# Two kinds of elementwise work of an encoder layer made on GpSimd instead of VectorE: a weight sum and the low parts of turned activations

## The chip, the cores and the metric

One core of a Trainium2 chip runs the whole program: TensorE (PE, with its weight loads as PEld), VectorE (DVE), ScalarE (ACT), GpSimd (POOL), and SyncE (SP), which issues the DMAs. The metric is the device time of one execution in microseconds, with inputs and outputs in HBM. Times of a run differ a little from execution to execution, so a change of the whole is judged by the median of several, and its stages by one profiled execution.

## The reference

Two layers of an encoder over 256 tokens of width 1024, all in float32. What matters here is how each layer's matmuls are made; the change touches the projection of attention and the FFN.

```python
q, k, v = ...                                   # normed, rotated
branch_b = gqa_attention(q, k, v) @ w_o_attn    # 1024 x 1024
mixed = jax.nn.sigmoid(gate_a) * branch_a + jax.nn.sigmoid(gate_b) * branch_b
h = h + rms_norm(mixed @ w_out, g_mix_post)

gate, up = jnp.split(rms_norm(h, g_ffn_pre) @ w_ffn_in, 2, axis=-1)   # FFN_HIDDEN = 2816
h = h + rms_norm((jax.nn.silu(gate) * up) @ w_ffn_out, g_ffn_post)
```

## The kernel before

**Three matmuls for one.** TensorE takes fp32r operands, so that each float32 operand is split into a high part (a cast on ACT) and a low part (source minus high part, a subtraction on DVE). `split` (L111) makes both, `mm3` (L99) adds three products: high by high, high by low, low by high. 12 matmuls of 512 columns make a half step of this, 24 a whole one.

**The weight stream.** Weights come in units of 128 x 2048 values. `plan` (L175) lists them in the order of use, and `Stream` (L214) loads them: raw buffers (two) by DMA on SP's queue, then for every unit two pieces of 1024 columns, each an ACT cast into `wh` (L113) and a DVE subtraction into `wl` (L109). There are four pairs of `wh` and `wl`, and `fill` (L309) prepares a unit as soon as fewer than `depth` pairs are held; `done` (L321) gives one back when its last matmul is recorded. A raw buffer can be loaded again when the DVE subtraction has read it.

**Groups of seven.** Where two halves of the tokens meet a 2 x 2 arrangement of weight units, seven products stand for eight (`seven`, L611, for the matmuls; `Stream.step`, L289, for the weights). `step` is called for n = 1 to 7 and each time makes one unit ready (`made`, L285). The four units of the group are x, z, y and q. x and z are loaded into a pair of `wh`/`wl` buffers lent for the purpose (tiles named `lent`), y into a large buffer (`big`), q into a raw buffer in step 5. Between the steps units are added to one another over 2048 columns by the helper `add` (L292):

| step | unit made ready | sum made after it, on DVE |
|---|---|---|
| 1 | x | x + z into x |
| 2 | x | x + y into x |
| 3 | x | |
| 4 | y | z + y into z |
| 5 | z | x + q into x |
| 6 | q | |
| 7 | x | |

There is one such group in each layer's merge (the attention projection; `MERGE`, L39) and three in each layer's FFN (`PAIRS`, L40), eight in all. The string `FFN` (L38) is the order of the FFN's steps: u a plain unit, a digit a step of the group of seven, o an output step, which needs the activations of one block of 256 hidden columns and one unit of `w_ffn_out`.

**Turned activations.** The FFN's hidden activations have to be transposed before the output steps. Most are turned by a DMA: `turn_words` (L394) takes each float32 word apart into two 16-bit halves (ACT copy, L404), sends it through a DMA transpose on SP's queue (L410), puts the halves together again (ACT copies, L417 and L423), and calls `Split.put` (L390), which splits the result into high and low part for `mm3`. `far=True` marks the calls from the FFN: in each layer four pieces of 256 columns (the first two blocks, by half of the tokens) and seven of 512 (three plain blocks, and two groups by half of the tokens). The last group's are turned on TensorE instead. `hid.need` makes the output step's matmuls wait until these parts have been recorded.

**Order.** The program's text is not the order of the engines' queues. The compiler orders each engine's instructions by priorities and by its own estimate of when their inputs are ready, so an instruction can stand in its queue well before the place where the text has it; `tc.issue_after` and `tc.high_priority` bend that order in places. On the chip each engine then runs its queue strictly in order and waits for semaphores. GpSimd's own work in the kernel is small: the powers and sums of the norms, the masks of the attention scores, the rope tables (L690, L694) and a few memsets.

Of the kernel before, what the change touches and what calls it, by code (L numbers as in the profile page):

```python
# [10 lines left out]
F32 = mybir.dt.float32  # L11
# [4 lines left out]
ALU = mybir.AluOpType  # L16
AX = mybir.AxisListType

P = 128
T = 256  # L20
# [31 lines left out]
def trunk_kernel(ctx: ExitStack, tc: tile.TileContext, a: dict, out: bass.AP):  # L52
# [7 lines left out]
    nc = tc.nc  # L60
# [13 lines left out]
    def nm(s):  # L74
        uid[0] += 1
        return f"{s}_{part[0]}_{uid[0]}"
# [4 lines left out]
    def mid(dt=F32):  # L81
        return b4p.tile([P, 1024], dt, tag="mid", name=nm("mid"))
# [7 lines left out]
    def t512():  # L90
        return smp.tile([P, 512], F32, tag="t512", name=nm("t512"), bufs=7)
# [16 lines left out]
    def vsub(out, in0, in1):  # L108
        nc.vector.tensor_tensor(out=out, in0=in0, in1=in1, op=ALU.subtract)  # L109

    def split(hi, lo, src):  # L111

        cast = nc.scalar.copy(hi, src)  # L113
        vsub(lo, src, hi.bitcast(F32))
        return cast
# [98 lines left out]
    class Stream:  # L214
# [54 lines left out]
        def put(self, x, parts=2):  # L269

            wh = wp.tile([P, UNIT], F32R, tag="wh", name=nm("wh"))
            wl = wp.tile([P, UNIT], F32R, tag="wl", name=nm("wl"))
            self.ready.append((wh, wl))
            self.held += 1
            cuts = [slice(j * x.n // parts, (j + 1) * x.n // parts) for j in range(parts)]
            return [(wh[:, c], wl[:, c], x.raw[:, c]) for c in cuts]
# [12 lines left out]
        def step(self, n, x, y, z, q):  # L289
            def add(to, other):  # L290
                c = slice(0, 2048)
                nc.vector.tensor_tensor(out=to.raw[:, c], in0=to.raw[:, c], in1=other.raw[:, c], op=ALU.add)  # L292

            if n == 7:
                self.load()
            self.made((x, x, x, y, z, q, x)[n - 1])
            if n == 1:
                add(x, z)
            elif n == 2:
                add(x, y)  # L300
            elif n == 4:
                add(z, y)
            elif n == 5:
                add(x, q)
            elif n == 7:
                self.held -= 1
                self.lend = True
# [55 lines left out]
    class Split:  # L363
# [23 lines left out]
                    kept.append(t)  # L387
            self.makers[hf] = kept

        def put(self, src, k, n, t0, tn):  # L390

            split(*self.at(k, n, t0, tn), src.rearrange("p (k t) -> p k t", t=tn))

        def turn_words(self, src, k, n, hf=None, far=False):  # L394

            x = lambda: t512()[:, : n * P * (2 if hf is None else 1)]
            w = x()
            w16 = w.bitcast(U16)
            nc.scalar.copy(  # L404
                w16.rearrange("p (s c) -> p s c", s=2), src.bitcast(U16).rearrange("p (c s) -> p s c", s=2)
            )
            yield SENT
            r, z = [t[:, : n * P * (2 if hf is None else 1)] for t in halves(mid())] if far else (x(), None)
            r16 = r.bitcast(U16)
            nc.sync.dma_start_transpose(out=r16.rearrange("p (r t) -> p r t", t=P), in_=w16)  # L410
            yield LANDED
            z = x() if z is None else z
            z16 = z.bitcast(U16)
            with tc.issue_after(ws.cast.ins) if far else nullcontext():
                if hf is None:
                    for i in range(2):
                        nc.scalar.copy(  # L417
                            z16.rearrange("p (k h t s) -> p h s k t", k=2, h=2, s=2)[:, i],
                            r16.rearrange("p (s h k t) -> p h s k t", h=2, k=2, s=2)[:, i],
                        )  # L420
                    self.put(z, k, n, 0, T)
                else:
                    nc.scalar.copy(z16.rearrange("p (c s) -> p s c", s=2), r16.rearrange("p (s c) -> p s c", s=2))  # L423
                    self.put(z, k, n, hf * P, P)

        def tok(self, k, hf):
            return [t[:, 0, :] for t in self.at(k, 1, hf * P, P)]
# [68 lines left out]
    def halves(t):  # L496
        return [t[:, j * 512 : (j + 1) * 512] for j in range(2)]
# [309 lines left out]
    for l in range(DEPTH):  # L807
# [222 lines left out]
        for x in range(2):  # L1030
            o = project_t(uT)
            for i in range(2):
                dst = qk[:, x, 2 * i : 2 * i + 2, :]
                src = o[i].rearrange("p (h t) -> p h t", t=T)
# [335 lines left out]
        for x in FFN:  # L1370
# [7 lines left out]
            if x == "o":  # L1378
                n, w = outs.pop(0), ws.take()
# [118 lines left out]
```

## Time and profile before

| | us |
|---|---|
| median of 3 runs | 920.66 |
| lowest and highest of them | 918.08, 2334.25 |
| the profiled execution | 919.17 |
| its span, from the first to the last instruction | 917.5 |

| engine in the profiled execution | busy us | share of the span | instructions |
|---|---|---|---|
| PE | 904.2 | 99% | 4561 |
| DVE | 769.0 | 84% | 963 |
| ACT | 643.6 | 70% | 1032 |
| POOL | 85.9 | 9% | 150 |

In rows of single instructions the columns are start, duration (both in us), engine, line, operation, output<-inputs, shapes and count; what stands in brackets is the engine's idle time before the instruction and what ended it. In rows of groups they are line, engine, operation, tiles, shapes and count, then busy us and mean ns of one, then idle time before. A row of a stretch has its borders and length, then the busy us and the number of instructions of PE, PEld, DVE, ACT and POOL, the granted TensorE clock, the DMA engines' share and GB/s. A row of the waits names who waited for whom, us in total, times, and the longest. Tile names carry the stage in which they were made: `wl_0ffnin` is a low weight part of layer 0's FFN. Matmuls overlap: each of 512 columns shows some 0.39 us, while the next begins 0.227 us after it.

### The profile page before, as it was taken

How to read it: one execution, taken by the hardware profiler on the slowest of the kernel's cores; microseconds unless marked ns; L12 is line 12 of the kernel's file. 1: busy time of each engine (PE TensorE's matmuls, PEld its weight loads, DVE VectorE, ACT ScalarE, POOL GpSimd, SP SyncE). 2: the span in 40 equal slices, each digit the busy share in tenths (PEclk: the TensorE clock that was granted, in tenths of full speed). 3: DMA queues.
4: the chain of work that ended last, by engine and by line, in shares of the span. 5: the costliest groups of instructions: out<-in, count | busy, mean ns of one | idle time of the engine just before them, and what ended most of it. 6: DMA issues, size and time to landing. Idle time of an engine off the chain costs nothing.

```text
span 917.5 us, 12250 instructions
## 1 busy us (share of the span) xinstructions
PE 904.2 (99%) x4561; PEld 767.2 (84%) x4561; DVE 769.0 (84%) x963; ACT 643.6 (70%) x1032; POOL 85.9 (9%) x150
## 2 busy tenths in 40 slices
PE   8999999999999999999999999999999999999996
PEld 7999888888878887888899988888888788888785
DVE  4798977988679998998689789699786799989874
ACT  4668778964668786776765686778566787967662
POOL 3400201040010000001023002100001000000000
PEclk9999999999999999999999999999999999999998
DMA  7464456657487676747445524394675957575541
GB/s 245 160 219 148 138 166 229 164 199 234 144 257 236 195 223 219 246 149 273 161 167 184 187 89 155 121 275 133 234 241 174 275 182 248 188 270 153 188 179 47
DMA packets 117786, 176.60 MB, mean 192 GB/s; under 512 B 33047, under 2 KB 56087, under 8 KB 117726
## 3 DMA queue, kind: packets, MB, share of 16 engines
q1 hardware_dynamic: 117726, 175.81, 59.1%
q8 instruction: 36, 0.59, 0.3%
q14 instruction: 24, 0.20, 0.1%
HBM read 167.41 MB, written 1.05 MB: 184 GB/s over the span
## 4 chain that ended last, share of the span: by engine, by line
PE 75%; DVE 11%; DMA 5%; ACT 4%; issue 3%; POOL 2%; SPq 0%; POOLq 0%; ACTq 0%; DVEq 0%
PE acc_0ffnin L97 10%; PE acc_1ffnin L97 6%; PE acc_1gate L97 5%; PE acc_0gate L97 5%; PE acc_0ffnin L577 4%; DVE wl_1ffnin L109 4%; PE acc_1gqk L97 3%; PE acc_0gqk L97 2%; PE acc_0rq L97 2%; PE acc_1ple L97 2%; PE acc_1gg L97 2%; PE acc_0gg L97 2%; PE acc_0v L97 2%; PE acc_1v L97 2%; PE acc_0merge L97 2%
## 5 line engine op out<-in xcount | busy, mean ns | idle before, releaser
L97 PE MATMUL acc_0ffnin<-wh_0ffnin,big_0ffnin 128*128 128x512 f32 x176 | 56.3, 392 | 0.0
L97 PE MATMUL acc_1ffnin<-wh_1ffnin,big_1ffnin 128*128 128x512 f32 x176 | 56.3, 392 | 0.0
L113 ACT CAST wh_1ffnin<-raw_1ffnin 128x1024 fp32r<-128x1024 f32 x38 | 38.4, 1050 | 17.8 <-DMA raw_1ffnin<-in_w_ffn_out_dram 13.6
L109 DVE TENSOR_TENSOR wl_1ffnin<-raw_1ffnin,wh_1ffnin 128x1024 fp32r<-128x1024 f32 x38 | 45.0, 1219 | 6.9 <-ACT wh_1ffnin L113 6.9
L113 ACT CAST wh_0ffnin<-raw_0ffnin 128x1024 fp32r<-128x1024 f32 x38 | 38.3, 1050 | 17.4 <-DMA raw_0ffnin<-in_w_ffn_out_dram 10.8
L109 DVE TENSOR_TENSOR wl_0ffnin<-raw_0ffnin,wh_0ffnin 128x1024 fp32r<-128x1024 f32 x38 | 45.0, 1220 | 5.9 <-ACT wh_0ffnin L113 5.9
L97 PEld LDWEIGHTS acc_0ffnin<-wh_0ffnin,big_0ffnin 128*128 128x128 f32 x176 | 33.0, 188 | 7.1 <-DVE big_0ffnin L109 0.2
L97 PEld LDWEIGHTS acc_1ffnin<-wh_1ffnin,big_1ffnin 128*128 128x128 f32 x176 | 33.0, 188 | 7.0 <-DVE big_1ffnin L109 0.2
L113 ACT CAST wh_0ffnin<-lent_0ffnin 128x1024 fp32r<-128x1024 f32 x30 | 30.2, 1050 | 9.0 <-DVE lent_0ffnin L292 3.4
L113 ACT CAST wh_1ffnin<-lent_1ffnin 128x1024 fp32r<-128x1024 f32 x30 | 30.2, 1051 | 8.8 <-PE acc_1ffnin L97 3.5
L109 DVE TENSOR_TENSOR wl_0ffnin<-lent_0ffnin,wh_0ffnin 128x1024 fp32r<-128x1024 f32 x30 | 35.3, 1219 | 1.2 <-ACT wh_0ffnin L113 1.2
L109 DVE TENSOR_TENSOR wl_1ffnin<-lent_1ffnin,wh_1ffnin 128x1024 fp32r<-128x1024 f32 x30 | 35.3, 1218 | 1.2 <-ACT wh_1ffnin L113 1.2
L97 PE MATMUL acc_0ffnin<-wl_0ffnin,big_0ffnin 128*128 128x512 f32 x88 | 34.4, 391 | 0.5 <-DVE wl_0ffnin L109 0.5
L97 PE MATMUL acc_1ffnin<-wl_1ffnin,big_1ffnin 128*128 128x512 f32 x88 | 34.5, 392 | 0.1
L577 PE MATMUL acc_1ffnin<-wh_1ffnin,mid_1ffnin 128*128 128x512 f32 x96 | 31.0, 390 | 0.0
L577 PE MATMUL acc_0ffnin<-wh_0ffnin,mid_0ffnin 128*128 128x512 f32 x96 | 31.0, 390 | 0.0
L97 PE MATMUL acc_1ffnin<-wh_1ffnin,big_1wout 128*128 128x512 f32 x96 | 30.4, 389 | 0.0
L97 PE MATMUL acc_0ffnin<-wh_0ffnin,big_0wout 128*128 128x512 f32 x96 | 30.3, 389 | 0.0
L97 PE MATMUL acc_0rq<-wh_start,big_start 128*128 128x384 f32 (+1 forms) x96 | 25.0, 345 | 0.6 <-ACT big_start L124 0.5
L97 PE MATMUL acc_1rq<-wh_0ple,big_0ple 128*128 128x384 f32 (+1 forms) x96 | 23.4, 325 | 0.0
L577 PE MATMUL acc_0ffnin<-wh_0ffnin,big_0wout 128*128 128x512 f32 x72 | 23.1, 389 | 0.0
L577 PE MATMUL acc_1ffnin<-wh_1ffnin,big_1wout 128*128 128x512 f32 x72 | 23.1, 389 | 0.0
(741 smaller groups left out, 3019.3 us busy)
## 6 DMA issues: line engine op xcount, KB each, us to landing
raw_0ffnin<-in_w_ffn_out_dram SPq DMA_DIRECT2D x11, 1024.0 KB, 5.4
raw_1ffnin<-in_w_ffn_out_dram SPq DMA_DIRECT2D x11, 1024.0 KB, 5.3
lent_0ffnin<-in_w_ffn_in_dram SPq DMA_DIRECT2D x6, 1024.0 KB, 7.6
lent_1ffnin<-in_w_ffn_in_dram SPq DMA_DIRECT2D x6, 1024.0 KB, 7.5
raw_0rq<-in_w_in_dram SPq DMA_DIRECT2D x4, 1024.0 KB, 5.1
raw_0v<-in_w_in_dram SPq DMA_DIRECT2D x4, 1024.0 KB, 5.1
raw_0merge<-in_w_out_dram SPq DMA_DIRECT2D x4, 1024.0 KB, 5.4
raw_0wout<-in_w_ffn_in_dram SPq DMA_DIRECT2D x8, 512.0 KB, 4.3
```

What stands on the lines that cost most here:

```text
L97: return nc.tensor.matmul(o, lhsT, rhs, start=start, stop=stop)
L109: nc.vector.tensor_tensor(out=out, in0=in0, in1=in1, op=ALU.subtract)
L113: cast = nc.scalar.copy(hi, src)
L577: nc.tensor.matmul(o, x, y, start=first and k + n == 0, stop=k == 3 and n == 2, skip_group_check=not first)
```

## The change

The sum z + y of each group of seven is no longer made on DVE in step 4. It is issued in step 1, behind x + z, on GpSimd and in two pieces of 1024 columns. And where a piece of activations was turned with `far=True`, its low part is subtracted on GpSimd; the high part stays an ACT cast. The other sums, the weights' low parts and all other splits stay on DVE.

```diff
             self.made((x, x, x, y, z, q, x)[n - 1])
             if n == 1:
                 add(x, z)
+                for c in (slice(0, 1024), slice(1024, 2048)):
+                    nc.gpsimd.tensor_tensor(out=z.raw[:, c], in0=z.raw[:, c], in1=y.raw[:, c], op=ALU.add)
             elif n == 2:
                 add(x, y)
-            elif n == 4:
-                add(z, y)
             elif n == 5:
                 add(x, q)
...
-        def put(self, src, k, n, t0, tn):
-
-            split(*self.at(k, n, t0, tn), src.rearrange("p (k t) -> p k t", t=tn))
+        def put(self, src, k, n, t0, tn, aside=False):
+
+            hi, lo = self.at(k, n, t0, tn)
+            src = src.rearrange("p (k t) -> p k t", t=tn)
+            if aside:
+                nc.scalar.copy(hi, src)
+                nc.gpsimd.tensor_tensor(out=lo, in0=src, in1=hi.bitcast(F32), op=ALU.subtract)
+            else:
+                split(hi, lo, src)
...
-                    self.put(z, k, n, 0, T)
+                    self.put(z, k, n, 0, T, far)
                 else:
                     nc.scalar.copy(z16.rearrange("p (c s) -> p s c", s=2), r16.rearrange("p (s c) -> p s c", s=2))
-                    self.put(z, k, n, hf * P, P)
+                    self.put(z, k, n, hf * P, P, far)
```

## The prediction

> **What bounds the kernel now.** I read the page's busy times first, then the same times cut into stretches of the kernel, then single instructions in order of time.
>
> ```profile
> PE 904.2 (99%) x4561; PEld 767.2 (84%) x4561; DVE 769.0 (84%) x963; ACT 643.6 (70%) x1032; POOL 85.9 (9%) x150
> ```
> ```profile
> 282.00:356.00 74.00, 73.55 (x325) 60.55 (x324) 71.88 (x69) 60.59 (x79) 0.00 (x0) 1.00 0.67 206
> 377.00:418.00 41.00, 41.00 (x185) 33.51 (x184) 38.78 (x36) 29.60 (x35) 0.96 (x1) 1.00 0.55 169
> 732.00:806.00 74.00, 73.86 (x326) 60.84 (x326) 72.16 (x69) 59.91 (x78) 0.00 (x0) 1.00 0.64 207
> 826.00:866.00 40.00, 39.79 (x180) 32.59 (x180) 37.33 (x34) 28.09 (x32) 0.00 (x0) 1.00 0.54 168
> ```
>
> PE is busy for 904.2 of 917.5 us, so the 84% of DVE (VectorE) is not what the end waits for: no edit that leaves the matmuls alone can win more than 13.3 us (1.4%), and the FFN, where most of this change lies, has little of that. The columns of the stretches are length, PE, PEld, DVE, ACT, POOL. 282 to 356 us holds the first two FFN groups of layer 0, 377 to 418 the third; the last two rows are the same of layer 1. PE loses 0.45, 0, 0.14 and 0.21 us in the FFN rows: 0.8 in all. That is the whole gain on offer there. But DVE stands at 97% between 282 and 356 (71.88 of 74), with GpSimd (POOL) empty beside it. **PE is the bound and DVE keeps up with nothing to spare**.
>
> **The change: what DVE gives up.** Rows of layer 0's FFN, by shape, then the end of the second group in order of time:
>
> ```profile
> L292 DVE TENSOR_TENSOR lent_0ffnin<-lent_0ffnin,big_0ffnin 128x2048 f32<-128x2048 f32 x6 | 13.7, 2285 | 0.0
> L109 DVE TENSOR_TENSOR big_0ffnin<-mid_0ffnin,big_0ffnin 128x512 fp32r<-128x512 f32 x7 | 4.8, 686 | 0.6 <-ACT big_0ffnin L113 0.6
> L109 DVE TENSOR_TENSOR big_0ffnin<-mid_0ffnin,big_0ffnin 128x256 fp32r<-128x256 f32 x4 | 1.7, 422 | 0.6 <-ACT big_0ffnin L113 0.6
> ```
> ```profile
> 330.16 2.29 DVE L292 TENSOR_TENSOR lent_0ffnin<-lent_0ffnin,lent_0ffnin 128x2048 f32<-128x2048 f32 x1
> 332.37 0.75 DVE L106 TENSOR_TENSOR t_0ffnin<-acc_0ffnin,t_0ffnin 128x256 f32<-128x256 f32 x2
> 333.03 2.29 DVE L292 TENSOR_TENSOR lent_0ffnin<-lent_0ffnin,big_0ffnin 128x2048 f32<-128x2048 f32 x1
> 335.23 2.36 DVE L109 TENSOR_TENSOR wl_0ffnin<-lent_0ffnin,wh_0ffnin 128x1024 fp32r<-128x1024 f32 x2
> ...
> 345.21 0.69 DVE L109 TENSOR_TENSOR big_0ffnin<-mid_0ffnin,big_0ffnin 128x512 fp32r<-128x512 f32 x1 [0.28 <-ACT big_0ffnin L113]
> ...
> 348.74 2.29 DVE L292 TENSOR_TENSOR lent_0ffnin<-lent_0ffnin,raw_0ffnin 128x2048 f32<-128x2048 f32 x1 [0.22 <-DMA raw_0ffnin<-in_w_ffn_in_dram]
> 350.95 0.69 DVE L109 TENSOR_TENSOR big_0ffnin<-mid_0ffnin,big_0ffnin 128x512 fp32r<-128x512 f32 x1
> 351.55 1.22 DVE L109 TENSOR_TENSOR wl_0ffnin<-raw_0ffnin,wh_0ffnin 128x1024 fp32r<-128x1024 f32 x1
> ...
> 353.82 2.35 DVE L109 TENSOR_TENSOR wl_0ffnin<-lent_0ffnin,wh_0ffnin 128x1024 fp32r<-128x1024 f32 x2
> ```
>
> Of the six `lent<-lent,big` adds three are z+y. From start to start, which is what a full queue pays, one takes 2.20 us (333.03 to 335.23), a low part of 512 columns 0.60 (350.95 to 351.55), one of 256 some 0.34 (0.422 less the same 0.08 of overlap). A layer's FFN gives up 3 x 2.20 + 7 x 0.60 + 4 x 0.34 = 12.2 us of DVE, and a merge group 2.2.
>
> **What GpSimd adds.** No row shows a GpSimd sum of 1024 columns. The nearest are the rope tables, also two-input sums from SBUF, met by DVE in two places:
>
> ```profile
> 21.29 0.33 POOL L694 TENSOR_TENSOR t_0rq<-mid_0rq 128x64 f32<-128x64 f32 x1
> 21.57 1.75 POOL L690 TENSOR_TENSOR t_0rq<-mid_0rq 128x256 f32<-128x256 f32 x1
> 24.95 0.60 POOL L694 TENSOR_TENSOR t_0rq<-mid_0rq 128x64 f32<-128x64 f32 x2
> 194.75 0.74 POOL L690 TENSOR_TENSOR t_0merge<-mid_0merge 128x256 f32<-128x256 f32 x1 [45.77 <-DMA mid_0merge<-in_g_q_norm_dram]
> 195.45 1.31 POOL L694 TENSOR_TENSOR t_0merge<-mid_0merge 128x64 f32<-128x64 f32 x1
> ```
> ```profile
> 17.01 1.26 DVE L124 TENSOR_TENSOR wl_start<-raw_start,wh_start 128x1056 fp32r<-128x1056 f32 x1 [0.55 <-ACT wh_start L124]
> 22.66 1.78 DVE L124 TENSOR_TENSOR wl_start<-raw_start,wh_start 128x1056 fp32r<-128x1056 f32 x1
> 24.36 1.28 DVE L124 TENSOR_TENSOR big_start<-aux_start,big_start 128x512 fp32r<-128x512 f32 x2
> 196.50 1.34 DVE L109 TENSOR_TENSOR wl_0merge<-raw_0gate,wh_0merge 128x1024 fp32r<-128x1024 f32 x1
> ```
>
> Alone, 64 columns take 0.33 us and 256 take 0.74: 2.14 ns a column, so 1024 would take 0.33 + 960 x 2.14 ns = 2.38 (estimate). Beside a busy DVE the 64 columns take 1.31, one whole DVE split: GpSimd gets its turn when the running DVE instruction ends. Then DVE pays: the split issued at 22.66 takes 1.78 instead of 1.26, 0.52 us lost to the 256 columns that end at 23.32, or 2.0 ns a column; after 64 columns a split takes 1.34 instead of 1.22, 1.9 ns a column. The two of 24.36 with one input in PSUM (`aux`) are not slowed by the GpSimd sums of 24.95. So **the two engines take turns when both read two SBUF operands**, and nearly all of DVE's work in these stretches is of that kind. I take 2.07 ns a column for the hold, between 2.0 and 2.14: 2.12 us for a piece of 1024, 1.06 and 0.53 for the low parts. Both ends: nothing (DVE never held) and the whole instruction (2.38, 1.29, 0.74).
>
> Held time per FFN: 6 x 2.12 + 7 x 1.06 + 4 x 0.53 = 22.3 us, less 12.2 given up: **DVE gets 10.1 us more to sit through in each layer's FFN, not less**, and 2.0 more per merge group.
>
> The Trainium skill (SBUF — State Buffer, section "Who interferes with whom") says that a DVE instruction with two SBUF inputs contends with a GpSimd instruction that reads SBUF, one waiting until the other is done. The kind agrees with 1.78 against 1.26; the length does not quite, since 0.52 of a 0.74 instruction was paid. By its rule the holds would be the whole instructions, the second rival below.
>
> **What of it reaches PE.** In order, by where DVE is late:
>
> ```profile
> 165.63 2.29 DVE L292 TENSOR_TENSOR lent_0gla<-lent_0gla,big_0gla 128x2048 f32<-128x2048 f32 x1
> 176.51 2.35 DVE L109 TENSOR_TENSOR wl_0merge<-raw_0gate,wh_0merge 128x1024 fp32r<-128x1024 f32 x2
> 317.96 1.23 DVE L109 TENSOR_TENSOR wl_0ffnin<-lent_0ffnin,wh_0ffnin 128x1024 fp32r<-128x1024 f32 x1 [1.25 <-ACT wh_0ffnin L113]
> 394.97 2.36 DVE L109 TENSOR_TENSOR wl_0ffnin<-big_0ffnin,wh_0ffnin 128x1024 fp32r<-128x1024 f32 x2
> ```
> ```profile
> 178.48 0.39 PE L97 MATMUL acc_0gate<-wh_0merge,big_start 128*128 128x512 f32 x1
> 351.99 0.39 PE L97 MATMUL acc_0ffnin<-wh_0ffnin,big_0ffnin 128*128 128x512 f32 x1
> 352.82 0.50 PE L97 MATMUL acc_0ffnin<-wl_0ffnin,big_0ffnin 128*128 128x512 f32 x1 [0.45 <-DVE wl_0ffnin L109]
> 397.01 0.39 PE L577 MATMUL acc_0ffnin<-wl_0ffnin,mid_0ffnin 128*128 128x512 f32 x1
> ```
>
> Merge: z+y already stands right behind x+z (165.63), so the two pieces take its place. The unit split at 176.51 is there whole at 178.87, while PE starts it at 178.48 and reaches its second half 12 matmuls on, 2.7 us later (0.227 from start to start): 2.3 us to spare against 2.0 more. Cost 0, and 0.5 if the hold is longer.
>
> First two FFN groups: the first adds 2.04 (4.24 - 2.20). The second adds 1.4, as its first piece runs beside the two `t<-acc` products at 332.37, which read PSUM. Three low parts of 256 and five of 512 fall here: 3 x 0.19 + 5 x 0.46 = 2.9. That is 6.3. The 1.25 us of idle at 317.96, where ACT waits for PE to free a weight buffer, takes its part, and the other 0.87 us of DVE's idle in the stretch (74 - 71.88 - 1.25, in gaps such as the 0.22 at 348.74) perhaps half. At 351.99 nothing is left to spare: PE waits there already, for DVE's split (0.83 from one matmul to the next). So 4.5 us come out of PE by 352.
>
> Third group: 2.0 for z+y and 0.9 for two low parts, against 0.9 us to spare at 397.01 (the first half of that unit is split by 396.11): 1.8 to 2. Layer 1 has the same order; PE lost 0.14 us in its first stretch where layer 0 lost 0.45, so I give it 0.3 more room in either place: 4.2 + 1.6. Sum: 4.5 + 1.9 + 4.2 + 1.6 = 12.2, **12 us**.
>
> Waits added: GpSimd's z+y waits for DVE's x+z (it overwrites what that reads) and for y's landing. Nothing queues behind it, as POOL's column is 0.00 in the FFN stretches except for one memset. z is split in step 5, in the second group at 353.82, 21 us after x+z ends, and two pieces with a DVE split's wait each are done in 7.2. Of the low parts those of the second group are read soonest: the one of 345.21 by the out step that PE begins at 351.99, 6 us later; on GpSimd it takes 2.5 with its wait. With that cover gone either would cost what it is late. ACT's casts and SP's DMA issues keep their number, but loads issue when DVE frees a raw buffer, so a late DVE makes late loads too:
>
> ```profile
> SPq L263 <- DVE wl_0ffnin L109: 72.3, 20, 10.3
> ```
>
> **The rivals.** *Relief without a hold*: GpSimd only fills what DVE leaves. For it:
>
> ```profile
> 101.15 4.05 POOL L1101 TENSOR_SCALAR_AFFINE_SELECT t_0gla<-t_0gla 128x256 f32<-128x256 f32 x1 [48.86 <-ACT t_0gla L1099]
> ```
> ```profile
> 102.57 2.35 DVE L109 TENSOR_TENSOR wl_0v<-raw_0gqk,wh_0v 128x1024 fp32r<-128x1024 f32 x2
> ```
>
> Here GpSimd sat through 4.05 us and DVE's splits ran at their usual 2.35 a pair. Against it: that is a one-input operation, and the two-input sums got in after every DVE split. It would return PE's 0.8 us: 919.2 - 0.8 = 918.4; with a partial hold up to 924.
>
> *DVE becomes the bound (slower)*: the hold is the whole GpSimd instruction, and as raw loads follow DVE, no idle of DVE but the two of 1.25 takes any of it. Per FFN 3 x (4.76 - 2.20) + 7 x 0.69 + 4 x 0.40 = 14.1, twice 28.2, less 2.5: 25.7, with a merge miss of 0.3 each: 945. It decides once the hold passes what the splits' margin of 1 to 3 us gives back between groups. Against it: 0.52 paid of 0.74, and DVE's idle between groups.
>
> *The change does not do what it says*: the order of instructions puts z+y late on GpSimd, and step 5's cast waits. Against it the 21 us. It costs 2 to 4 us a group, 935 to 950.
>
> **How the numbers follow.** The profiled execution took 919.17 us, 1.7 over its span; the runs' median is 920.66, lowest 918.08. I build on the profiled one: 919.2 + 12 = **931**. Chances: forecast (925 to 938) 0.62; relief 0.22; DVE bound 0.12; late z+y 0.04. Two per cent (902.2 to 939.1) is about what a measurement here tells from no change. Range 918 to 940: it takes in the relief and leaves out most of the last two. Over 2% faster: 0.01, as PE has 1.4% to give; slower: 0.12 and a part of the forecast's and the late z+y's tails, 0.15; within: 0.84.
>
> **What would show it.** GpSimd about 2.4 us alone and 3.5 beside a split for a piece; splits next to it at up to 3.3 us instead of 1.22; DVE's busy time up although it has fewer instructions; PE waits for `wl_0ffnin`/`wl_1ffnin` of some 6 us a layer, none in merge. Splits that stay at 1.22 make me wrong downward; late raw loads between groups, upward.

## The result, and the profile after

The changed kernel takes 944.71 us (median; 942.70 to 947.36), the kernel before 920.71 beside it: ratio 1.0269, interval 1.0248 to 1.0290. One of the four executions of the kernel before took 2334.25 us and is left out of the ratio. The forecast was 931, with a range of 918 to 940. The profiled execution of the change took 946.44 us with a span of 944.7. The busy times of its page:

```profile
PE 913.5 (97%) x4561; PEld 770.9 (82%) x4561; DVE 787.8 (83%) x933; ACT 644.1 (68%) x1032; POOL 171.2 (18%) x188
```

DVE has 30 instructions fewer and 18.8 us more. The groups of POOL and single instructions of DVE and POOL in the first two FFN groups show why (a pair of splits that nothing holds takes 2.35):

```profile
L300 POOL TENSOR_TENSOR lent_0ffnin<-lent_0ffnin,big_0ffnin 128x1024 f32<-128x1024 f32 x6 | 17.6, 2950 | 40.7 <-DVE lent_0ffnin L292 40.7
...
L396 POOL TENSOR_TENSOR big_0ffnin<-mid_0ffnin,big_0ffnin 128x512 fp32r<-128x512 f32 x7 | 12.6, 1795 | 35.0 <-ACT big_0ffnin L395 35.0
```
```profile
290.90 6.06 POOL L300 TENSOR_TENSOR lent_0ffnin<-lent_0ffnin,big_0ffnin 128x1024 f32<-128x1024 f32 x2 [2.28 <-DVE lent_0ffnin L292]
...
291.29 6.75 DVE L109 TENSOR_TENSOR wl_0ffnin<-raw_0ffnin,wh_0ffnin 128x1024 fp32r<-128x1024 f32 x2
...
338.17 2.41 POOL L300 TENSOR_TENSOR lent_0ffnin<-lent_0ffnin,big_0ffnin 128x1024 f32<-128x1024 f32 x1 [6.89 <-DVE lent_0ffnin L292]
```

Two GpSimd sums make a pair of splits 4.40 us longer: **2.20 us of hold for 1024 columns**, where the forecast said 2.12. A sum that DVE hardly keeps waiting takes 2.41 (forecast 2.38): the one at 338.17 begins beside DVE's products that read PSUM and before 0.45 us in which DVE stands idle. The two engines take turns, and the size of a hold was forecast within 4%.

PE's waits for the same kernel (total, times, longest, in us), and the two FFN stretches of layer 0 that answer to 282 to 356 and 377 to 418 of before:

```profile
PE acc_1ffnin L97 <- DVE wl_1ffnin L109: 6.1, 3, 2.9
PE acc_0ffnin L97 <- DVE wl_0ffnin L109: 6.0, 3, 2.9
PE aux_1ffnin L442 <- DVE t_1ffnin L106: 2.0, 1, 2.0
...
PE acc_1gate L97 <- DVE wl_1merge L109: 1.4, 2, 1.0
PE aux_0ffnin L442 <- DVE t_0ffnin L106: 1.3, 1, 1.3
...
PE acc_0gate L97 <- DVE wl_0merge L109: 1.0, 1, 1.0
```
```profile
284.40:366.40 82.00, 77.03 (x325) 62.42 (x325) 77.96 (x59) 60.84 (x79) 26.52 (x13) 0.96 0.67 201
387.40:431.30 43.90, 41.14 (x184) 33.37 (x184) 39.73 (x31) 29.03 (x34) 9.56 (x5) 1.00 0.49 154
```

The waits of 6.0 and 6.1 us are those that the forecast named, in their size too. The borders are moved by what PE is late there, so that the matmuls are the same (325, and 184 of 185). The first stretch is 8.0 us longer than before though, and PE idles for only 5.0 of its 82.0. The column behind POOL, the granted clock, tells the rest: 0.96 instead of 1.00. Behind the longest wait:

```profile
349.60 0.79 PE L97 MATMUL acc_0ffnin<-wl_0ffnin,big_0ffnin 128*128 128x512 f32 x1 [2.87 <-DVE wl_0ffnin L109]
```
```profile
346.50:349.50 3.00, 0.22 (x1) 0.00 (x0) 3.00 (x3) 2.13 (x3) 1.96 (x1) 0.88 0.00 0
348.80:355.60 6.80, 6.00 (x14) 4.75 (x15) 6.80 (x6) 6.58 (x9) 1.43 (x2) 0.50 0.55 180
349.60:355.30 5.70, 5.70 (x13) 4.45 (x14) 5.70 (x5) 5.67 (x8) 1.32 (x1) 0.50 0.60 193
```

The clock is granted at 0.50 from 348.80 on, while PE still waits, and up to 355.60: behind the wait of 2.87 us, 13 matmuls run in 5.7 us where 25 would fit at 0.227. In the whole run 23 matmuls of 512 columns follow the one before at 0.427 us: 23 x 0.2 = 4.6 us that no row calls a wait.

Where the time went, by the first PE instruction of each stage (change against before, us; the kernels of the last two columns come below). Ahead of these stretches, up to layer 0's gate, the three differ from before by -0.4, +0.2 and +0.5.

| stretch | forecast | the change | with x + q behind z's split | the same, z + y alone |
|---|---|---|---|---|
| layer 0, merge and output projection | 0 | +2.9 | +1.3 | +1.3 |
| layer 0, FFN up to its last transposes | 6.4 | +10.8 | +7.8 | +3.9 |
| on to layer 1's gate | 0 | +1.0 | -0.2 | -0.2 |
| layer 1, merge and output projection | 0 | +2.2 | +1.2 | +1.2 |
| layer 1, FFN up to its last transposes | 5.8 | +9.5 | +8.3 | +4.3 |
| from there to the end | 0 | +1.3 | -0.6 | -0.7 |

### The profile page after: what moved, and what is told of

The parts are those of the page before. It is cut to its first block, busy times and chain, and to the rows that moved or that the text cites. A ratio compares the mean times of both kernels' runs of the same rounds, so it can differ in the third digit from the quotient of the medians.

```text
span 944.7 us, 12295 instructions
## 1 busy us (share of the span) xinstructions
PE 913.5 (97%) x4561; PEld 770.9 (82%) x4561; DVE 787.8 (83%) x933; ACT 644.1 (68%) x1032; POOL 171.2 (18%) x188
## 4 chain that ended last, share of the span: by engine, by line
PE 45%; DVE 20%; issue 13%; ACT 9%; DMA 9%; POOL 3%; SPq 0%; POOLq 0%; ACTq 0%; DVEq 0%
PE acc_0ffnin L97 9%; DVE wl_1ffnin L109 6%; PE acc_1ffnin L97 6%; DVE wl_0ffnin L109 3%; PE acc_0ffnin L583 3%; PE acc_0gqk L97 2%; PE acc_0rq L97 2%; PE acc_1ple L97 2%; PE acc_0v L97 2%; PE acc_1merge L97 2%; PE acc_0gg L97 2%; DVE wl_0gate L109 2%; DVE wl_0merge L109 2%; PE acc_1rq L97 1%; ACT wh_1ffnin L113 1%
## 5 line engine op out<-in xcount | busy, mean ns | idle before, releaser
L97 PE MATMUL acc_1ffnin<-wh_1ffnin,big_1ffnin 128*128 128x512 f32 x176 | 58.7, 405 | 0.0
L109 DVE TENSOR_TENSOR wl_1ffnin<-raw_1ffnin,wh_1ffnin 128x1024 fp32r<-128x1024 f32 x38 | 52.2, 1411 | 7.7 <-ACT wh_1ffnin L113 7.6
L109 DVE TENSOR_TENSOR wl_0ffnin<-raw_0ffnin,wh_0ffnin 128x1024 fp32r<-128x1024 f32 x38 | 52.2, 1412 | 6.8 <-ACT wh_0ffnin L113 6.8
L109 DVE TENSOR_TENSOR wl_0ffnin<-lent_0ffnin,wh_0ffnin 128x1024 fp32r<-128x1024 f32 x30 | 45.3, 1545 | 2.4 <-ACT wh_0ffnin L113 2.3
L109 DVE TENSOR_TENSOR wl_1ffnin<-lent_1ffnin,wh_1ffnin 128x1024 fp32r<-128x1024 f32 x30 | 45.3, 1544 | 2.1 <-ACT wh_1ffnin L113 2.0
L113 ACT CAST wh_1ffnin<-lent_1ffnin 128x1024 fp32r<-128x1024 f32 x30 | 30.3, 1049 | 10.1 <-DVE lent_1ffnin L292 4.8
L97 PE MATMUL acc_1ffnin<-wh_1ffnin,big_1wout 128*128 128x512 f32 x96 | 30.4, 389 | 0.0
L97 PE MATMUL acc_0ffnin<-wh_0ffnin,big_0wout 128*128 128x512 f32 x96 | 30.4, 389 | 0.0
L396 POOL TENSOR_TENSOR big_0ffnin<-mid_0ffnin,big_0ffnin 128x512 fp32r<-128x512 f32 (+1 forms) x11 | 17.6, 1604 | 63.4 <-ACT big_0ffnin L395 63.4
L396 POOL TENSOR_TENSOR big_1ffnin<-mid_1ffnin,big_1ffnin 128x512 fp32r<-128x512 f32 (+1 forms) x11 | 17.7, 1613 | 62.7 <-ACT big_1ffnin L395 62.7
L300 POOL TENSOR_TENSOR lent_0ffnin<-lent_0ffnin,big_0ffnin 128x1024 f32<-128x1024 f32 x6 | 17.6, 2950 | 40.7 <-DVE lent_0ffnin L292 40.7
```

Of the source, the lines that this page charges most:

```text
L97: return nc.tensor.matmul(o, lhsT, rhs, start=start, stop=stop)
L300: nc.gpsimd.tensor_tensor(out=z.raw[:, c], in0=z.raw[:, c], in1=y.raw[:, c], op=ALU.add)
L396: nc.gpsimd.tensor_tensor(out=lo, in0=src, in1=hi.bitcast(F32), op=ALU.subtract)
```

## The experiments

**The two parts alone.** z + y on GpSimd without the low parts, and the low parts without z + y (each the diff of the change with the other half taken out).

> Only the z+y sums are on GpSimd; the low parts of the turned activations stay on DVE. Theory A (DVE and GpSimd take turns when both read two SBUF operands, and PE waits where a held split is due): 934 to 940 us, most of the 24 us of the whole change; splits of 3.4 us behind each GpSimd piece, PE waits of about 2 us in the first FFN group and 3 in the second, with a stretch at half the granted clock behind the longer one. Theory B (the moved place in the queues and the waits for GpSimd cost the time, not the reading): also 930 to 940, but with splits at 1.22 us. Theory C (the low parts carry it, since an out step waits for them): 921 or less.

> Only the low parts of the turned activations are on GpSimd; z+y stays on DVE in step 4. Theory A: DVE sits through 7 x 0.46 + 4 x 0.19 = 4.0 us more in each layer's FFN and has about 2 us of idle to take it: 921 to 926. Theory B: 920 to 922. Theory C: 930 or more.

z + y alone takes 939.28 us, 1.0206 (1.0173 to 1.0239); the low parts alone 927.09, 1.0077 (1.0049 to 1.0104). The sum of both, 2.8%, is the whole change's 2.7%: they add up. z + y is the large part, with 13.7 us more DVE time. The low parts, 1 us above theory A's range, add 4.1 us to each layer's FFN up to the transposes, where the forecast's terms for them are 2.9 + 0.9. But PE's waits for `wl` are only 2.6 and 2.1 of that; 1.3 and 2.0 are waits of the last transposes for `t`, for which the forecast had no term.

**No reading, and one reading.** z + y on GpSimd as in the first run, but z's two pieces are only written (z is set to a constant), or only z is read (z times 1); y is not added in either.

```diff
-nc.gpsimd.tensor_tensor(out=z.raw[:, c], in0=z.raw[:, c], in1=y.raw[:, c], op=ALU.add)
+nc.gpsimd.memset(z.raw[:, c], 0.5)                                    # the one
+nc.gpsimd.tensor_scalar(out=z.raw[:, c], in0=z.raw[:, c], scalar1=1.0, scalar2=0.0, ...)   # the other
```

> As e1_sums, with the same order on every engine, but each GpSimd piece only writes a constant over its 1024 columns of z instead of adding y (the sum z+y is left out, so step 5's weights are wrong). GpSimd waits for x+z as before and reads nothing. Theory A: no split is held, DVE has 2.2 us a group less to do: 917 to 921, splits at 1.22. Theory B: within 3 us of e1_sums, as every wait and every place in the queues is the same.

> As e1_sums, but each GpSimd piece reads and writes z alone (z times 1 plus 0; y is not added, so step 5's weights are wrong). Theory A in the form that two operands on both sides are needed: 917 to 922, as the one-input mask of before let DVE's splits run at their usual time. Theory A in the form that any GpSimd reading holds a two-input split for as long as it reads: between 922 and e1_sums, with splits of 1.22 plus the piece's time. Theory B: as e1_sums.

918.72 us, 0.9992 (0.9977 to 1.0007), and 919.87, 1.0002 (0.9988 to 1.0016). Writing alone, and reading z alone, in the same stretch of group 1 (two rows each, of the two kernels):

```profile
288.31 1.85 POOL L300 MEMSET lent_0ffnin<- 128x1024 f32 x2 [26.19 <-DVE lent_0ffnin L292]
...
289.05 2.35 DVE L109 TENSOR_TENSOR wl_0ffnin<-raw_0ffnin,wh_0ffnin 128x1024 fp32r<-128x1024 f32 x2
```
```profile
288.24 2.55 POOL L300 TENSOR_SCALAR lent_0ffnin<-lent_0ffnin 128x1024 f32<-128x1024 f32 x2 [25.86 <-DVE lent_0ffnin L292]
...
289.79 3.20 DVE L109 TENSOR_TENSOR wl_0ffnin<-raw_0ffnin,wh_0ffnin 128x1024 fp32r<-128x1024 f32 x2
```

Writing holds nothing (2.35). One reading holds the low part of 256 columns ahead of the pair and the pair itself, 0.84 + 0.85 us for two pieces, about 0.85 for 1024 columns: less than the 2.20 of two readings. Neither form of theory A had this: the split is held, but for less than the GpSimd instruction's time. The first run also prices what DVE gives up: DVE is rid of z + y for nothing (752.3 us busy, 769.0 before), and the kernel gains nothing. Relief alone was never worth more than PE's few waits.

**The order of x + y, and shorter pieces.** In groups 2 and 3 of the changed kernel x + y stands ahead of both raw splits, in the kernel before between them. The first run holds it back until the first half of the next unit is split; the second makes z + y in eight pieces of 256 columns; the third does both. All three have the whole change.

```diff
-                add(x, y)
+                self.late = lambda: add(x, y)        # issued behind the next unit's first split
```
```diff
-for c in (slice(0, 1024), slice(1024, 2048)):
+for c in [slice(i, i + 256) for i in range(0, 2048, 256)]:
```

> The whole change, but x+y of step 2 is held in DVE's queue behind the first split of the unit that follows, as it stood before (333 to 341 us of before: split, split, first split of the next unit, x+y). In the changed kernel x+y runs ahead of that split in the second and third FFN groups, and PE waits 3.0 and 1.6 us for it, the longer wait with 2.6 us of half granted clock behind it. If the lost time comes from this place in the queue: 2.2 us a group earlier, the long waits go below 1 us, 934 to 938 us. If it comes from the held time alone, the debt is the same wherever x+y stands: 942 to 946.

> The whole change, with z+y on GpSimd in eight pieces of 256 columns instead of two of 1024. Held time in all is the same (2048 columns), but a DVE split sits through 0.5 us at a time instead of 2.2, so that two splits in a row lose 1.1 and not 4.4 and the rest of the debt falls on later ones. If a long hold just ahead of PE's due time costs the waits: the first group's 1.8 us wait and the merge's 1.2 go mostly, 930 to 938. If the sum of held time alone counts: 942 to 947.

> Both: pieces of 256 columns and x+y behind the next unit's first split. If both count, about 925 to 932, near the net of 10 us a layer less DVE's idle; if neither does, 942 to 947.

946.19, 945.27 and 944.70 us; ratios 1.0289 (1.0257 to 1.0321), 1.0278 (1.0251 to 1.0305), 1.0269 (1.0240 to 1.0297). Neither the place of x + y nor the length of one hold makes the loss; the columns that are read do.

**Half of it, and plain DVE work instead.** Half of z + y on GpSimd; then no GpSimd work, and one more DVE operation of 2048 or 1024 columns in step 4; then z + y on GpSimd in the merge groups alone.

```diff
+nc.gpsimd.tensor_tensor(out=z.raw[:, :1024], ...)     # half: columns 1024 to 2048 stay in step 4 on DVE
```
```diff
             elif n == 4:
                 add(z, y)
+                c = slice(0, 2048)                     # or 1024
+                nc.vector.tensor_tensor(out=z.raw[:, c], in0=z.raw[:, c], in1=z.raw[:, c], op=ALU.max)
```

> Only the first 1024 columns of each z + y are made on GpSimd; the other 1024 stay a DVE sum in step 4, and the low parts stay on DVE. Each of the 8 groups then holds DVE for some 2.20 us and gives back 1.1, half of what the run with all of z + y on GpSimd has; that run had 13.7 us more DVE time and 20 us more in all. Theory A, nothing absorbs DVE's extra time (one us of it costs the end about one us, and long waits of PE add a little through the granted clock): 926 to 930, half of the other run's loss. Theory B, the margins that the prediction counted are there, some 3 us per FFN and 2 per merge group, and only what passes them costs: 1.1 per merge group and 3.3 per FFN are within them, 918 to 921. The splits beside a piece should show 3.4 us for a pair of halves' one, as before, and there should be 8 such holds.

> Nothing is on GpSimd that was not there before; behind z + y in step 4 DVE makes one more sum-like operation of 2048 columns per group, max(z, z), which leaves z as it is. DVE gets 8 x 2.2 = 17.6 us more work and no holds. Theory A, DVE's time costs the end about one for one wherever it comes from: 937 to 942, about what z + y on GpSimd took (939), and PE waits for the weights' low parts in the same places; if waits of 2 to 3 us are what halves the granted clock, it falls here too, without a busy GpSimd. Theory B, margins of some 3 us per FFN and 2 per merge absorb the first of it: 924 to 928. Theory C, the turn-taking on SBUF does harm that DVE's busy time does not show (to ACT, to DMAs, to PE): then plain DVE work of the same size costs clearly less than 939 and the clock stays at full speed.

> As the run with max(z, z) of 2048 columns, but of 1024: 8 x 1.1 = 8.8 us more DVE work. Theory A (one for one): 928 to 931, half of the other's loss. Theory B (margins first): 919 to 921, since 1.1 per merge group and 3.3 per FFN fit in them. A and B differ in shape here: under A the two runs lie on a line through the time before, under B the first 1024 columns cost nothing and the second 1024 all of it.

> z + y is made on GpSimd in the two merge groups alone (the first and the fifth group of the kernel); the six FFN groups and the low parts are as before. It tests the prediction's term for the merge, 0 because the unit's second half had 2.3 us to spare: 4.4 held less 2.2 given up in each. The prediction's step: 919 to 921 and no wait of PE for a low part in the gate. Theory A (nothing to spare, as the first half of that unit has only about 1 us and what is late there stays late): 922 to 925, with a wait of PE of 1 to 1.4 us for wl in each gate.

Half takes 929.36 us, 1.0108 (1.0085 to 1.0132): half of the loss, as theory A has it. Plain DVE work takes 926.50, 1.0073 (1.0049 to 1.0098), with 2048 columns and 919.97, 1.0003 (0.9990 to 1.0015), with 1024: theory B's figures; the first also fits theory C, a harm of the turn-taking beyond DVE's time. So A falls, but B does not stand either, since the half ran into a loss where it had room. The merge alone takes 923.80, 1.0043 (1.0028 to 1.0058), theory A's figure, and its waits are nearly those of the change:

```profile
PE acc_1gate L97 <- DVE wl_1merge L109: 1.0, 1, 1.0
PE acc_0gate L97 <- DVE wl_0merge L109: 1.0, 1, 1.0
```

**DVE work in the place of the holds, and holds in the place of step 4.** Four operations max(z, y) of 1024 columns on DVE behind x + z, z + y left out; and z + y on GpSimd begun in step 4, alone and with the whole change.

```diff
             if n == 1:
                 add(x, z)
+                for c in (slice(0, 1024), slice(1024, 2048)) * 2:
+                    nc.vector.tensor_tensor(out=z.raw[:, c], in0=z.raw[:, c], in1=y.raw[:, c], op=ALU.max)
```

> No GpSimd work is added. Right behind x + z in step 1, where GpSimd's two pieces held DVE, DVE itself makes four operations of 1024 columns, max(z, y), some 4.5 us; z + y in step 4 is left out, so that z is not the sum (b11, b12 and b22 go in otherwise; this part of the result is not computed). DVE's net work per group is that of the run with max(z, z) of 2048 columns in step 4, which took 926.5: 2.2 us more. Theory D, the place decides: 4.4 us at once behind x + z find a margin of 1 to 1.4 us in the next unit, and the 2.2 us given back in step 4 come after PE has waited: 936 to 941, as with z + y on GpSimd (939), with PE waits of 2 to 3 us. Theory C, turn-taking on SBUF harms beyond DVE's time: 924 to 928, as the other run of the same net work. Theory A (every net us costs one wherever it is) has fallen with the runs at 920 and 926.5 and is not asked again.

> z + y on GpSimd in its two pieces, low parts on DVE as before, but begun in step 4 and not in step 1: a GpSimd sum of one column that reads the low part of y's unit is put ahead of the two pieces and makes them wait for that split. Number, size and kind of the holds are those of the run that took 939: 16 of some 2.2 us. Theory D (place): the holds now fall where DVE has been relieved of z + y (2.2 us) and the next halves have 2 to 3 us to spare; 919 to 925, with DVE's busy time up by some 14 us all the same. Theory C (harm of the turn-taking itself): 936 to 941. A rival of its own: z's split in step 5 then waits for GpSimd, and comes 1 to 3 us late, up to 930.

> The whole change with z + y begun in step 4 as in the run beside it: low parts of turned activations on GpSimd too. Those alone took 927. Theory D: 926 to 932, 13 to 19 us less than the change as it was made, with not one hold less. Theory C: 942 to 947. It also tells whether the two parts still add up.

The first takes 930.92 us, 1.0123 (1.0108 to 1.0138), between both theories. In group 1 it does to PE what the holds do. DVE and PE of this kernel, and PE of the changed one:

```profile
292.32 4.62 DVE L300 TENSOR_TENSOR lent_0ffnin<-lent_0ffnin,big_0ffnin 128x1024 f32<-128x1024 f32 x4
...
298.47 0.50 PE L97 MATMUL acc_0ffnin<-wl_0ffnin,big_0wout 128*128 128x512 f32 x1 [1.59 <-DVE wl_0ffnin L109]
```
```profile
298.10 0.50 PE L97 MATMUL acc_0ffnin<-wl_0ffnin,big_0wout 128*128 128x512 f32 x1 [1.67 <-DVE wl_0ffnin L109]
```

The other two (940.55, 1.0223; 944.71, 1.0276) test nothing: the compiler put the gate behind the sums on GpSimd, so that they are repeats of z + y alone and of the change, and agree with these.

Reading the queues of all these kernels side by side showed what had been mixed up. x + q of step 5 stands **ahead of the raw unit's split** (in group 3, of y's) in the kernel before, in the change and in the run of 939; in the FFN groups of the three runs with more DVE work the compiler had moved it behind that split, in two of them behind z's. Theory E came from that.

**The place of x + q.** z + y alone, the whole change, and last the kernel before, each with x + q behind z's split; and z + y begun in step 4 with a gate that z + y depends on.

```diff
             elif n == 5:
-                add(x, q)
+                with tc.issue_after(self.low.ins):     # z's second DVE split
+                    add(x, q)
```

> z + y on GpSimd behind x + z as in the run of 939; the one difference is that DVE's x + q of step 5 stands behind the split of z instead of ahead of the raw unit's split (in group 3 ahead of y's). That is where it stands in the run with DVE work in the place of the holds, which took 930.9. Theory E, the order: an x + q ahead of a raw unit's split makes that split 2.2 us later, its raw buffer is free 2.2 us later, and the load that waits for the buffer lands later, so that DVE's idle time behind it absorbs nothing: 929 to 934, with fewer waits of PE in the second and third group, while the wait behind x + z (some 2 us in the first group) stays. Theory C, taking turns harms beyond the order and DVE's time: 937 to 941.

> The whole change, with x + q behind the split of z as in the run beside it. Theory E: 933 to 939, some 8 us under the change as it was made. Theory C: 942 to 947.

> z + y on GpSimd, begun for certain behind y's split of step 4: two GpSimd operations of two columns first (the low part of y's unit less itself, and that nought added to z's columns 1023 and 1024), which both pieces of z must wait for. x + q stays ahead of the raw unit's split. Theory D (place): no wait behind x + z any more, 2 us less in each first group, and the holds fall beside x + q and the raw unit's split, where z + y was taken off DVE before: 925 to 932. If the holds cost the same wherever they stand: 937 to 941. If z's split waits for GpSimd: PE waits for wl of step 5, 930 to 942.

> The kernel before, with nothing on GpSimd, and x + q behind z's split as in the run of 929.9. In the kernel before x + q stands ahead of the raw unit's split too (in group 3 ahead of y's), as in the change. Theory E, the place of x + q makes room only for a DVE that is late: PE is on time here but for some 2 us in the second and third groups, so 917.5 to 920.5, the same or up to 0.2% faster. If the place of x + q were worth 8 to 9 us by itself, and the runs with it were cheaper for that alone: 910 to 913. If it were to break something else: above 922.

z + y alone falls from 939.28 to 929.88 us, 1.0106 (1.0088 to 1.0123), the whole change from 944.71 to 936.95, 1.0174 (1.0150 to 1.0198). Theory E's figures, with the same holds (32.8 against 32.5 us of DVE time over the usual durations, with z + y alone). What it does in group 2: DVE's queue with SP's load, first of z + y alone, then with x + q behind.

```profile
355.67 2.29 DVE L292 TENSOR_TENSOR lent_0ffnin<-lent_0ffnin,raw_0ffnin 128x2048 f32<-128x2048 f32 x1 [0.34 <-DMA raw_0ffnin<-in_w_ffn_in_dram]
...
358.48 2.35 DVE L109 TENSOR_TENSOR wl_0ffnin<-raw_0ffnin,wh_0ffnin 128x1024 fp32r<-128x1024 f32 x2
...
367.06 3.50 DVE L109 TENSOR_TENSOR wl_0ffnin<-raw_0ffnin,wh_0ffnin 128x1024 fp32r<-128x1024 f32 x3 [3.36 <-ACT wh_0ffnin L113]
...
360.86 0.37 SPq L263 DMA_DIRECT2D raw_0ffnin<-in_w_ffn_out_dram  x1
```
```profile
354.95 2.36 DVE L109 TENSOR_TENSOR wl_0ffnin<-raw_0ffnin,wh_0ffnin 128x1024 fp32r<-128x1024 f32 x2 [0.26 <-ACT wh_0ffnin L113]
...
359.61 2.29 DVE L293 TENSOR_TENSOR lent_0ffnin<-lent_0ffnin,raw_0ffnin 128x2048 f32<-128x2048 f32 x1
...
363.62 2.36 DVE L109 TENSOR_TENSOR wl_0ffnin<-raw_0ffnin,wh_0ffnin 128x1024 fp32r<-128x1024 f32 x2 [1.12 <-ACT wh_0ffnin L113]
...
357.34 0.37 SPq L263 DMA_DIRECT2D raw_0ffnin<-in_w_ffn_out_dram  x1
```

The load is issued 0.03 us after the raw split ends (358.48 + 2.35, 354.95 + 2.36), and the split that waits for it begins 6.2 to 6.3 us after the issue in both. With x + q ahead DVE makes its sum first and then stands idle for 3.36 us; with x + q behind, the load is on its way while the sum is made, and 1.12 are left. DVE's idle time ahead of a raw unit is no room that a late DVE can use: the idle time moves with it. Here x + q behind makes it room.

This room is not the whole gain. With z + y alone, 20 matmuls at the half clock (4.0 us) are gone as well. In the whole change PE's waits for `wl` stay at 6.0 us in each FFN with x + q behind; what goes are the transposes' waits (1.3 and 2.0 become 0 and 0.7), 9 of the 23 slow matmuls, and 2.6 us in the merges and output projections. And 929.88 is about what DVE work of the holds' size took in their place, with x + q behind as well in the FFN (930.92): theory C falls, a hold costs in all what as much DVE work costs.

The true late start takes 945.95 us, 1.0260 (1.0221 to 1.0298), above all three ranges. Its holds fall on a low part and on the raw unit's splits ahead of step 5. POOL and DVE of this kernel:

```profile
305.89 7.17 POOL L306 TENSOR_TENSOR lent_0ffnin<-lent_0ffnin,big_0ffnin 128x1024 f32<-128x1024 f32 x2
...
307.93 2.90 DVE L109 TENSOR_TENSOR big_0ffnin<-mid_0ffnin,big_0ffnin 128x512 fp32r<-128x512 f32 x1
310.75 4.53 DVE L109 TENSOR_TENSOR wl_0ffnin<-raw_0ffnin,wh_0ffnin 128x1024 fp32r<-128x1024 f32 x2
```

But z is now late for step 5. ACT's casts of z wait for GpSimd's sums, 13.0 us in layer 0's FFN and 13.4 in layer 1's, and in group 3 a copy that PE needs (L635) stands behind them in ACT's queue. ACT and PE:

```profile
403.14 1.05 ACT L113 CAST wh_0ffnin<-lent_0ffnin 128x1024 fp32r<-128x1024 f32 x1 [4.13 <-POOL lent_0ffnin L306]
...
407.04 0.50 PE L582 MATMUL acc_0ffnin<-wh_0ffnin,mid_0ffnin 128*128 128x512 f32 x1 [3.19 <-ACT mid_0ffnin L635]
```

So this run pays for a new wait, the last of the outcomes named ahead of it, and does not say what the holds would cost in that place alone.

The kernel before with x + q behind takes **917.86 us, 0.9966 (0.9953 to 0.9980)**: the place of x + q is worth 0.3% where DVE is on time and 0.9 to 1.0% where it is held. The first is a little more than theory E's 0.2%. This version beats both kernels; with z + y or the low parts on GpSimd none did. The busy times of its page:

```profile
PE 903.6 (99%) x4561; PEld 768.2 (84%) x4561; DVE 770.5 (84%) x963; ACT 643.5 (70%) x1032; POOL 84.3 (9%) x150
```

## Why the prediction was wrong, step by step

**The bound** was right: PE at 99%, nothing to win. Relief for nothing, in the run that only writes, changed the time by -0.1%.

**What GpSimd adds** was right: 2.20 us of hold per 1024 columns against 2.12, 2.41 alone against 2.38. The rule of the Trainium skill (SBUF — State Buffer, section "Who interferes with whom"), by which one of the two waits until the other is done, gives the kind again; the trace puts the hold at 2.20 beside instructions of 2.4 to 3.4. Over the whole kernel DVE's busy time rose by 18.8 us, less than the forecast's 2 x 10.1 + 2 x 2.0 = 24.2; some sums begin where DVE is idle or reads PSUM, as at 338.17. That nothing queues behind the sums was wrong, since the low parts do (one of 256 columns at 296.93, behind 290.90 + 6.06), but PE has no wait for GpSimd in the stages of the change.

**What of it reaches PE** is the step that failed, and it failed in what the forecast put at 0 or had no term for. The term that it did work out came true: PE's waits for `wl` in the FFN are 1.67 + 2.87 = 4.5 us in layer 0's first two groups (forecast 4.5) and 1.5 in the third (1.9), 4.5 and 1.6 in layer 1 (4.2 and 1.6).

*The merge, at 0.* It costs 1.4 to 2.0 us in each group when made alone, 4.2 in the median, and 2.9 and 2.2 with the output projection in the change. I had measured the unit's second half (2.3 to spare) and read past the first. PE needs its low part at 178.71, and it is split at 177.73 (176.51 + 1.22): 0.98 to spare against 2.0, and PE waits 1.03. PE before, then DVE and PE of the change:

```profile
178.71 0.39 PE L97 MATMUL acc_0gate<-wl_0merge,big_start 128*128 128x512 f32 x1
```
```profile
178.21 2.36 DVE L109 TENSOR_TENSOR wl_0merge<-raw_0gate,wh_0merge 128x1024 fp32r<-128x1024 f32 x2
...
179.48 0.50 PE L97 MATMUL acc_0gate<-wl_0merge,big_start 128*128 128x512 f32 x1 [1.03 <-DVE wl_0merge L109]
```

*The granted clock.* No term. 23 matmuls at half speed are 4.6 us of the change, 20 are 4.0 with z + y alone; with x + q behind z's split 14 and none are left. The profile before, without one such wait, could not show it. The Trainium skill has a rule that I did not weigh (TensorE: Matmul & The Clock Gate, section "HAM oscillation — how this bites in real kernels"): no gaps of PE above about 3.4 us. Here gaps of 2.9 were enough, and one of 2.0.

*The end of each FFN*, at 0. The last group's transposes wait 1.3 and 2.0 us for their `t` products, as they also do with the low parts alone.

*Idle time, counted as room.* That the waits for `wl` come out as forecast is in part luck, since neither part alone keeps to its terms. These leave 2.6 us for z + y in layer 0's FFN and 2.0 in layer 1's (6.4 and 5.8 less 3.8 for the low parts). z + y alone cost 7.6 and 9.5; PE's waits for `wl` are 5.1 and 5.3 of that. I had netted a group's 4.24 us of hold against the 2.20 given up, and taken the idle times off the rest. But in group 1 the hold comes at once behind x + z, and the kernel before made z + y there at 294.20 at the earliest (DVE of before):

```profile
288.66 2.35 DVE L109 TENSOR_TENSOR wl_0ffnin<-raw_0ffnin,wh_0ffnin 128x1024 fp32r<-128x1024 f32 x2
...
294.20 2.28 DVE L292 TENSOR_TENSOR lent_0ffnin<-lent_0ffnin,big_0ffnin 128x2048 f32<-128x2048 f32 x1
```

The unit split there, at 291.29 in the change, is the one of PE's wait at 298.10; it is late before DVE gives anything up or has any idle time, and the 1.25 us at 317.96 come 20 us too late for it. In the merge and in groups 2 and 3 z + y stood next behind x + z in the kernel before as well (165.63, 333.03, 379.97), and there the net fits: in the merge DVE is 2.1 us late (178.21 against 176.51, with PE 0.42 earlier). The idle time elsewhere moves with DVE, since loads follow its splits: in the first stretch DVE idled for 2.1 us before (74.00 - 71.88) and for 4.0 after (82.00 - 77.96). The sentence stood in my own prediction, in the rival ("as raw loads follow DVE"); in the forecast I counted the idle time as room all the same. With x + q behind, where some room exists, z + y costs 3.9 and 4.3.

Against the profiled execution (946.4, forecast 931.2) some 15 us are missing. By the table, 5.1 are in the merges and output projections, 4.4 + 3.7 in the FFNs and 2.3 behind them. Of the 8.1 in the FFNs the transposes' waits are 3.3 and the clock 3.8 (19 of the 23 matmuls). These overlap: a late load in one stage is a longer wait and a slower clock in the next.

**The rivals.** "DVE becomes the bound", 945, came out within 0.3 us, at a chance of 0.12, and by luck: its price for a hold, the whole instruction, is too high, it knew nothing of the clock, and it put 25.7 us into the FFNs and 0.3 into each merge, where the table has 20.3 and 5.1. Its reason, that idle time absorbs little because raw loads follow DVE, agrees with the runs on x + q. "Relief without a hold" falls with the hold. "Late z + y" is not what happened, since the sums begin right behind x + z (POOL's 2.28 us of idle time at 290.90 end with it); where they were made to begin late, ACT's casts did wait for them, and the kernel took 945.95.

**Left open.** DVE work of the holds' size behind x + z cost 11 us (930.92) and in step 4 7 us (926.50), both with x + q behind the raw split in the FFN. So place seems to count, but these are single kernels whose queues differ in more than that place, and the one run that moved GpSimd's sums brought a new wait. Why the output projections are slower by 1 to 2 us than PE's wait in the merge explains was not followed up.

## What to carry to other kernels

Idle time of an engine is room only if what ends it does not depend on that engine: look at when the load that ends it was issued, and by whose end. Net a cost against a saving only as far as the saving comes first; otherwise compare the gross delay with the margin at the very next consumer, and for its first half. Give every stage that the change touches its own row before its term is put at 0. Moving work to an engine that holds the first one while it reads pays only when the hold per column is shorter than the time saved, here 2.15 ns against 1.07.

## What the runs showed of the hardware

GpSimd's effect on DVE's two-input instructions goes by what it reads from SBUF: two readings hold DVE for 2.20 us per 1024 columns, one for about 0.85, writing alone for nothing; cutting the work into pieces of 256 columns hardly changes the sum (DVE 785.7 us busy against 787.8). The granted clock fell to half at each of the nine waits of PE of 2.8 us or more in these runs, at 16 of the 25 between 1.8 and 2.6 us (at one of 1.81 and not at one of 1.84 of the same run, z + y alone) and at none of the shorter ones, start and end of the kernel left out. It stayed there for 3.4 us, in three cases for 6.8.
